# Both directions of a delta rule head solved in one product of 128 rows

## The chip, the cores and the metric

One core of a Trainium2 chip. The metric is the device time of one launch in microseconds. The core has a matrix engine (TensorE, PE in the profile, with its weight loads as PEld), a vector engine (DVE), an activation engine (ACT), GpSimd (POOL), and a queue that issues most DMAs (SP). TensorE writes to PSUM only, from which DVE and ACT read.

## The reference, cut to what matters

One encoder layer over two sequences of 256 tokens (512 rows, 1024 channels, f32): RMSNorm, one wide projection, three branches (a bidirectional gated delta rule with 8 heads of 128, latent attention with 8 heads, cross attention into 256 memory tokens), their gated sum, an output projection and a last RMSNorm. The change touches the delta rule, which each head computes in both directions:

```python
lmat = einsum("nbhck,nbhek->nbhce", kb, kc) * decay * (1.0 - eye)
t_inv = triangular_solve(lmat + eye, eye)        # unit lower triangular
u = einsum("nbhce,nbhev->nbhcv", t_inv, vc * bc)
w = einsum("nbhce,nbhek->nbhck", t_inv, kb * exp(gc))
...
v_new = u_i - w_i @ state
o = (q_i * exp(g_i)) @ state + (q_i k_i^T * decay_i) @ v_new
state = state * exp(g_last) + (k_i * exp(g_last - g_i))^T @ v_new
...
o_gdn = rmsnorm(o_fwd + o_bwd) * silu(z)
```

The backward direction is the same on the reversed sequence. The kernel does not go chunk by chunk with a state: it solves the triangular system of a whole sequence of 256 tokens by blocks and multiplies the result (`ub`) with the decayed products of q and k.

## The kernel before, in words

`run` (L1210) has three stages. `front` computes the memory branch, the norms, the projections and the latent attention. `middle` computes the delta rule heads while TensorE works through projections. `back` computes the last branch product (`gm_bg`) and the output (`y`). Long products are `gemm` (L220): f32 inputs are split into two rounded parts, and three products of 128x128 by 128x512 for each slice of 128 input channels give one output tile. Each weight tile comes by a DMA (`wr`), is copied on ACT (`wh`) and subtracted on DVE or GpSimd (`wl`), with two buffers each.

In `middle` the order of TensorE's instructions is written by hand: `weave` (L1375) runs several generators against a clock of its own. Each `yield a, b` says that the generator has just issued `a` us of TensorE work and wants to go on `b` us later; until then `weave` issues instructions of the long products (`self.fill`), 0.234 us each. The instructions of the other engines are placed by the compiler's scheduler; every engine takes its own in order. The generators are `preps` (two of `gdn_prep`, each for four heads), `heads_load` and `heads_in` (decays, products of k and q), two of `lane` (even and odd heads; each runs `gdn_solve` for its heads, one after the other) and `heads_out` (`gdn_out`). `can` holds back the fill work whose inputs are not there; `load_xa` brings the attention branch's results back from DRAM into buffers of the solve that have come free.

The solve of a head has 256 tokens in two chunks of 128 for each of two sequences (`s`) and two directions (`d`). `gdn_prep` inverts diagonal blocks of 32 on DVE. With them `gdn_solve` (L912) makes inverses of 64:

- `p1` and `yp` (L933, L944), each 16 products of 32x32, give the corner blocks between two inverses of 32; ACT copies `p1` to `p1s` and `yp` into `y64` (L954). The forward direction has its first half in partitions 0 to 63 and its second in 64 to 127; the backward direction has them the other way round.
- Then for `cp` 0 and 1 (first and second chunk of a direction): `u` (L984) multiplies the inverse of the first half by its part of v, ACT copies it into `ub` (L988), `xs` (L997) multiplies the block between the halves (from `na`) by it, DVE subtracts that from v (`w2`, L1001), `us` (L1009) multiplies by the second half's inverse, ACT copies into `ub` (L1013). Each of the three is four products of 64x64 by 64x128, one for each sequence and direction, with the directions on different quarters of the array.
- Between `cp` 0 and 1, `x` (L973), four products of 128x128 by 128x128, and a subtraction from v on DVE (L976).

All of these products are in f32, not split. `vt` (`vs` in the profile) is the head's v, loaded from DRAM by one DMA (L845) and scaled by `nk` (L908). `y64` has, for each direction, sequence and chunk, 64 rows of an inverse in each partition half; its four copies from `o1` and `o2` (L827) mask one half with `hm`.

Of the kernel before, what the change touches and what calls it, by code (L numbers as in the profile page):

```python
# [40 lines left out]
def _consts():  # L41
    t = np.arange(P)
    b = t // 32
    same = b[:, None] == b[None, :]
    le = t[:, None] <= t[None, :]
    ge = t[:, None] >= t[None, :]
    z, o = np.zeros((P, P)), np.ones((P, P))
    a8 = np.arange(8)
    anc = np.zeros((P, 2, 2, 8))
    for tb in range(2):  # L50
        tg = tb * P + t
        anc[:, 0, tb] = tg[:, None] >= 32 * a8[None]
        anc[:, 1, tb] = tg[:, None] < 32 * (a8[None] + 1)
    i32 = np.arange(32)
    m = (t % 32)[:, None]
    parts = [
        ("id", np.eye(P)), ("bd", same),
        ("anc", anc.reshape(P, 32)),
        ("trf", m <= i32), ("trb", m >= i32), ("i32", m == i32),
        ("ngf", np.where(i32 > m, 0.0, NEG)), ("ngb", np.where(i32 < m, 0.0, NEG)),  # L60
        ("hm", np.stack([b % 2 == 0, b % 2 == 1], 1)),
        ("one", np.ones((P, 1))), ("hf", np.full((P, 64), -0.5)), ("ph", np.full((P, 16), 0.5)),
    ]
# [92 lines left out]
class Layer:  # L156
# [558 lines left out]
    def gdn_prep(self, g, kqs):  # L715
# [58 lines left out]
        nc.vector.tensor_scalar(nk, nk, 0.25, None, ALU.mult)  # L774
        self.cn[g] = cc, nk
# [40 lines left out]
        y64 = pg.tile([P, 32, 64], F32, tag="y64", bufs=2, name=f"y64{g}")  # L816
# [6 lines left out]
        for d in range(2):  # L823
            u = slice(16 * d, 16 * d + 16)
            ysrc = o1 if d else o2
            for hf in range(2):
                nc.scalar.activation(y64[:, u, 32 * hf:32 * hf + 32], ysrc[:, :, u].rearrange("p i u -> p u i"),  # L827
                                     AF.Copy, scale=c("hm")[:, hf:hf + 1])
                if g:
                    yield 0.0, 2.5  # L830
        self.ready[g] = self.now + (10 if g else 80)
        return t32, y64, cc

    def decay_in(self, hh):
        nc, pg = self.nc, self.pg

        es = []
        for d in range(2):
            e = pg.tile([P, 2, 384], F32, tag="e", bufs=6, name=f"e{hh}{d}")
            for a in range(4):  # L840
                src = self.d_r[d, 4 * hh + a:4 * hh + a + 1].rearrange("a s i -> a (s i)")
                nc.sync.dma_start(e[32 * a:32 * a + 32].rearrange("p s i -> p (s i)"), src.to_broadcast([32, 768]))
            es.append(e)
        vt = self.s2(f"vs{hh}")
        nc.sync.dma_start(vt, self.d_v[:, hh])  # L845
        return es, vt
# [65 lines left out]
    def gdn_solve(self, hh):  # L912

        nc, pg, c = self.nc, self.pg, self.c
        t32, y64, cc = self.pr[hh // 4]
        h, par = hh % 4, hh % 2
        na, es, vt = self.hd[hh]
        v4 = vt.rearrange("p (s c d) -> p s c d", s=2, c=2)

        def ncol(d, s, cch):  # L920

            cp = cch if d == 0 else 1 - cch
            return (256 if cp else (128 if d else 0))
# [3 lines left out]
        for j in range(4):  # L927
            s, cch = j // 2, j % 2
            for m in range(2):
                for d in range(2):  # L930
                    f, sb = (2 * m + 1, 2 * m) if d else (2 * m, 2 * m + 1)
                    n0 = ncol(d, s, cch) + 32 * sb
# [3 lines left out]
        p1s = pg.tile([P, 128], F32, tag="p1", bufs=2, name=f"p1s{hh}")  # L936
# [3 lines left out]
        for j in range(4):  # L940
            for m in range(2):
                for d in range(2):
                    f, sb = (2 * m + 1, 2 * m) if d else (2 * m, 2 * m + 1)
                    nc.tensor.matmul(yp[32 * f:32 * f + 32, 32 * j:32 * j + 32],  # L944
                                     p1s[32 * sb:32 * sb + 32, 32 * j:32 * j + 32],
                                     y64[32 * sb:32 * sb + 32, 16 * d + 4 * h + j, 32 * (1 - d):32 * (1 - d) + 32],
                                     start=True, stop=True)
        for d in range(2):
            for m in range(2):
                f = 2 * m + 1 if d else 2 * m  # L950
                r = slice(32 * f, 32 * f + 32)
                dst = y64[r, 16 * d + 4 * h:16 * d + 4 * h + 4, 32 * (1 - d):32 * (1 - d) + 32]
                src = yp[r, 0:128].rearrange("p (j i) -> p j i", j=4)
                nc.scalar.activation(dst, src, AF.Copy)  # L954
# [4 lines left out]

        def half(d, first):  # L960
            return slice(64, 128) if (d == 1) == first else slice(0, 64)

        for cp in range(2):
            def vin(d, r):
                return v4[r, :, d if cp == 0 else 1 - d]

            if cp == 1:
# [7 lines left out]
                for d in range(2):  # L975
                    nc.vector.tensor_tensor(v4[:, :, 1 - d], v4[:, :, 1 - d], x4[:, d], op=ALU.subtract)  # L976
                yield 0.9, 5.0
            up = self.ps_ms(par, f"u{hh}{cp}")
            u3 = up[:, 0:256].rearrange("p (s e) -> p s e", s=2)
            for s in range(2):  # L980
                for d in range(2):
                    r = half(d, True)
                    cch = cp if d == 0 else 1 - cp
                    nc.tensor.matmul(u3[r, s], y64[r, 16 * d + 4 * h + 2 * s + cch], vin(d, r)[:, s],  # L984
                                     start=True, stop=True)
            for d in range(2):
                r = half(d, True)
                nc.scalar.activation(ub[r, d, :, cp], u3[r], AF.Copy)  # L988
            yield 0.58, 5.0
            xp = self.ps_ms(par, f"xs{hh}{cp}")  # L990
            x3 = xp[:, 0:256].rearrange("p (s e) -> p s e", s=2)
            for s in range(2):
                for d in range(2):
                    f, sb = half(d, True), half(d, False)
                    cch = cp if d == 0 else 1 - cp
                    n0 = ncol(d, s, cch) + sb.start
                    nc.tensor.matmul(x3[sb, s], na[f, d, s, n0:n0 + 64], ub[f, d, s, cp], start=True, stop=True)  # L997
            w2 = pg.tile([P, 2, P], F32, tag=f"w2{par}", bufs=1, name=f"w2{hh}{cp}")
            for d in range(2):
                sb = half(d, False)  # L1000
                nc.vector.tensor_tensor(w2[sb], vin(d, sb), x3[sb], op=ALU.subtract)  # L1001
            yield 0.58, 5.0
            up = self.ps_ms(par, f"us{hh}{cp}")
            u3 = up[:, 0:256].rearrange("p (s e) -> p s e", s=2)
            for s in range(2):
                for d in range(2):
                    sb = half(d, False)
                    cch = cp if d == 0 else 1 - cp
                    nc.tensor.matmul(u3[sb, s], y64[sb, 16 * d + 4 * h + 2 * s + cch], w2[sb, s],  # L1009
                                     start=True, stop=True)  # L1010
            for d in range(2):
                sb = half(d, False)
                nc.scalar.activation(ub[sb, d, :, cp], u3[sb], AF.Copy)  # L1013
            yield 0.58, 5.0
        self.ub[hh] = ub

    def gdn_out(self, hh):
# [29 lines left out]
        yield 0.0, 9  # L1047
# [193 lines left out]
    def plan(self):  # L1241
# [12 lines left out]
        xa = [(f, n) for n in range(5) for f in (self.load_xa, self.split_xa)]  # L1254
# [65 lines left out]
    def middle(self):  # L1320
# [5 lines left out]
        nc.vector.memset(self.tt.rearrange("p a b -> p (a b)")[:, 0:1024:33], 1.0)  # L1326
        self.loads, self.loaded, self.started = {}, {}, set()
# [38 lines left out]
    def can(self, f, *a):  # L1366

        if f == self.load_xa:
            return (3 in self.ub and self.pr[1], 5 in self.ub and 7 in self.hd, 6 in self.ub and 7 in self.hd,
                    self.out > 6 and 7 in self.started, 7 in self.ub)[a[0]]  # L1370
# [58 lines left out]
    def load_xa(self, part):  # L1429

        lo, hi = ((0, 2), (2, 3), (3, 4), (4, 5), (5, 8))[part]
        ts = []
        while lo + len(ts) < hi:
            f = lo + len(ts)
            if f in (0, 6):
                t = self.pg.tile([P, 2, 2, 512], F32R, tag="y64", bufs=2, name=f"xa{f}")
                ts += [t[:, 0], t[:, 1]]
            else:
                t, n = ("ub", 2) if f == 4 else ("na", 3)
                ts.append(self.pg.tile([P, 2, 512], F32R, tag=t, bufs=n, name=f"xa{f}"))  # L1440
        for f, t in enumerate(ts, lo):
            self.nc.sync.dma_start(t[:, 1].bitcast(F32), self.d_xa[:, f])
        self.xa_at[part] = self.now + 6.0 if part < 4 else self.now
# [33 lines left out]
```

## Time and profile before

| | before |
|---|---|
| time, median of 3 runs | 902.44 us (900.96 to 902.75) |
| profiled execution, its own time | 902.51 us |
| its span, first to last instruction | 900.6 us |
| granted TensorE clock, mean | 0.993 |
| busy: PE, PEld, DVE, ACT, POOL | 98%, 78%, 65%, 48%, 22% |

How to read it: the shares are of the span, over all stages. The name of a product is its output tile, with the line that issued it; `gm_` names are the long products. An instruction's duration for PE runs from its start to its modelled end, and the next one starts before that end; what an instruction costs in a busy stream is the difference between starts. An f32 product stands as two MATMUL records, a split one as one. Some matmul records can be missing, so a row may count one fewer than were issued.

### The profile page before, as it was taken

How to read it: one execution, taken by the hardware profiler on the slowest of the kernel's cores; microseconds unless marked ns; L12 is line 12 of the kernel's file. 1: busy time of each engine (PE TensorE's matmuls, PEld its weight loads, DVE VectorE, ACT ScalarE, POOL GpSimd, SP SyncE). 2: the span in 40 equal slices, each digit the busy share in tenths (PEclk: the TensorE clock that was granted, in tenths of full speed). 3: DMA queues.
4: the chain of work that ended last, by engine and by line, in shares of the span. 5: the costliest groups of instructions: out<-in, count | busy, mean ns of one | idle time of the engine just before them, and what ended most of it. 6: DMA issues, size and time to landing. Idle time of an engine off the chain costs nothing.

```text
span 900.6 us, 13529 instructions
## 1 busy us (share of the span) xinstructions
PE 879.4 (98%) x5100; PEld 706.2 (78%) x5100; DVE 584.3 (65%) x988; ACT 432.0 (48%) x769; POOL 197.9 (22%) x146
## 2 busy tenths in 40 slices
PE   7999999999999999999989998999999999999997
PEld 5878886888888888887867776777777778888886
DVE  6775447876678774489979995575655445336642
ACT  6655445554554544364375368555553333213332
POOL 0230341222122200060230232431220000332221
PEclk9999999999999999999989999999999999999999
DMA  9322211532335433364322345443432337455422
GB/s 333 115 86 84 90 58 52 160 103 89 97 96 150 138 103 121 117 188 142 126 97 83 129 129 152 143 122 124 129 107 96 100 102 242 163 183 207 123 96 94
DMA packets 47520, 114.03 MB, mean 127 GB/s; under 512 B 6496, under 2 KB 9696, under 8 KB 47456
## 3 DMA queue, kind: packets, MB, share of 16 engines
q1 hardware_dynamic: 42704, 104.52, 36.7%
q10 hardware_dynamic: 4752, 8.65, 2.6%
q8 instruction: 40, 0.66, 0.3%
q14 instruction: 24, 0.20, 0.1%
HBM read 93.03 MB, written 16.97 MB: 122 GB/s over the span
## 4 chain that ended last, share of the span: by engine, by line
PE 91%; ACT 4%; DVE 1%; DMA 1%; issue 1%; POOL 0%; SPq 0%; POOLq 0%; ACTq 0%; DVEq 0%
PE gm_g L232 15%; PE gm_qkv L232 14%; PE gm_z L232 6%; PE gm_bm L232 5%; PE gm_bg L232 5%; PE gm_za L232 5%; PE y L1158 5%; PE vm L359 3%; PE gm_be L232 3%; PE gm_qm L232 3%; PE gm_km L232 2%; PE kk L895 2%; PE s_a L282 2%; PE o L1034 2%; PE gm_cq L232 2%; PE gm_qn L232 2%
## 5 line engine op out<-in xcount | busy, mean ns | idle before, releaser
L205 POOL TENSOR_TENSOR wl_qkv<-wr_qkv,wh_qkv 128x1024 fp32r<-128x1024 f32 x24 | 59.7, 2489 | 152.9 <-ACT wh_qkv L201 49.7
L686 DVE SCALAR_TENSOR_TENSOR kq<-cz,prm,kq 128x510 f32<-128x510 f32 (+1 forms) x64 | 55.2, 862 | 10.3 <-ACT kq L679 9.4
L232 PE MATMUL gm_qkv<-hh,wh_qkv 128*128 128x512 f32 x192 | 52.3, 408 | 0.1
L232 PE MATMUL gm_qkv<-hh,wl_qkv 128*128 128x512 f32 x192 | 52.2, 406 | 0.0
L232 PE MATMUL gm_g<-hh,wh_g 128*128 128x512 f32 x192 | 51.7, 403 | 0.0
L232 PE MATMUL gm_g<-hh,wl_g 128*128 128x512 f32 x192 | 51.4, 399 | 0.0
L232 PE MATMUL gm_g<-hl,wh_g 128*128 128x512 f32 x192 | 51.0, 400 | 0.0
L232 PE MATMUL gm_qkv<-hl,wh_qkv 128*128 128x512 f32 x192 | 50.6, 399 | 0.0
L1128 POOL TENSOR_TENSOR mg<-mg,lg 128x512 f32<-128x512 f32 x16 | 28.0, 1749 | 75.9 <-DVE lg L1127 75.9
L205 DVE TENSOR_TENSOR wl_g<-wr_g,wh_g 128x1024 fp32r<-128x1024 f32 x24 | 29.9, 1247 | 22.4 <-ACT wh_g L201 11.0
L232 PEld LDWEIGHTS gm_qkv<-hh,wh_qkv 128*128 128x128 f32 x192 | 36.0, 193 | 9.8 <-issue 0.9
L885 POOL TENSOR_TENSOR kl<-kq,kh 128x512 fp32r<-128x512 f32 x16 | 20.7, 1296 | 101.4 <-ACT kh L883 101.4
L232 PEld LDWEIGHTS gm_qkv<-hl,wh_qkv 128*128 128x128 f32 x192 | 35.6, 188 | 9.3 <-issue 1.1
L232 PEld LDWEIGHTS gm_g<-hl,wh_g 128*128 128x128 f32 x192 | 35.7, 188 | 9.0 <-issue 0.9
L232 PEld LDWEIGHTS gm_g<-hh,wl_g 128*128 128x128 f32 x192 | 35.8, 188 | 8.8 <-issue 0.7
L232 PEld LDWEIGHTS gm_g<-hh,wh_g 128*128 128x128 f32 x192 | 35.4, 189 | 8.8 <-issue 1.0
L232 PEld LDWEIGHTS gm_qkv<-hh,wl_qkv 128*128 128x128 f32 x192 | 35.8, 192 | 8.2 <-issue 0.3
L1158 PE MATMUL y<-wh_wo,mh 128*128 128x512 f32 (+1 forms) x144 | 39.7, 368 | 0.0
L201 ACT ACTIVATE wh_g<-wr_g 128x1024 fp32r<-128x1024 f32 x24 | 25.4, 1057 | 27.2 <-PE gm_g L232 19.3
L201 ACT ACTIVATE wh_qkv<-wr_qkv 128x1024 fp32r<-128x1024 f32 x24 | 25.4, 1057 | 23.8 <-PE gm_qkv L232 6.5
L798 DVE TENSOR_TENSOR tm<-xx,tt 128x1 f32<-128x1 f32 (+30 forms) x62 | 34.7, 560 | 1.3
L232 PE MATMUL gm_bm<-xa,wh_bm 128*128 128x512 f32 x128 | 32.6, 397 | 0.0
(396 smaller groups left out, 2220.6 us busy)
## 6 DMA issues: line engine op xcount, KB each, us to landing
wr_qkv<-in_w_dram SPq DMA_DIRECT2D x24, 512.0 KB, 3.5
wr_g<-in_w_dram SPq DMA_DIRECT2D x24, 512.0 KB, 3.6
e<-d_r SPq DMA_DIRECT2D x64, 96.0 KB, 3.0
wr_z<-in_w_dram SPq DMA_DIRECT2D x12, 512.0 KB, 3.9
wr_za<-in_w_dram SPq DMA_DIRECT2D x8, 512.0 KB, 3.5
d_g<-gt_g ACTq DMA_DIRECT2D x16, 256.0 KB, 2.1
wr_bm<-in_w_dram SPq DMA_DIRECT2D x8, 512.0 KB, 3.6
lg<-d_g SPq DMA_DIRECT2D x16, 256.0 KB, 3.5
```

What stands on the lines that cost most here:

```text
L201: nc.scalar.activation(hi[:, :n], raw[:, :n], AF.Copy)
L205: eng.tensor_tensor(lo[:, :n], raw[:, :n], hi[:, :n].bitcast(F32), op=ALU.subtract)
L232: nc.tensor.matmul(ps[:m], a[:, k * m:(k + 1) * m], xs[k][j], start=n == 0, stop=n == 3 * nk - 1)
L282: nc.tensor.matmul(sp[:, qb * 256:(qb + 1) * 256], a, b, start=j == 0, stop=j == n - 1)
L359: nc.tensor.matmul(vps[tb], ms[k][a][:, t], b[:, :512], start=k == 0 and i == 0, stop=k == 7 and i == 2)
L686: nc.vector.scalar_tensor_tensor(ys, zs, self.cw[:, f, m:m + 1], ys, ALU.mult, ALU.add)
L798: nc.vector.tensor_tensor(t3, xx[:, i:i + 1, 0:i].to_broadcast([P, i, i]), tt[:, 0:i, 0:i], op=ALU.mult)
L885: nc.gpsimd.tensor_tensor(lo, src, hi.bitcast(F32), op=ALU.subtract)
L895: nc.tensor.matmul(ps, a[:, k], b, start=i == 0, stop=i == 2)
L1034: nc.tensor.matmul(out, ub[:, d, s, cp], rhs, start=n == 0, stop=n == 3)
L1128: nc.gpsimd.tensor_tensor(self.merged[d], self.merged[d], gt, op=ALU.add)
L1158: nc.tensor.matmul(ps, xs[2 * j + q][a][:, t], b[:, q * 512 + c0:q * 512 + c1], start=j == 0 and n == 0, stop=j == 3 and n == 5)
```

## The change

The two directions are put into one operand. A tile `y` of 128x128 per sequence and chunk holds, on its diagonal, the 64x64 inverse of the forward direction's first half (partitions 0 to 63) and of the backward direction's first half (64 to 127); a second one holds the second halves. The rest of `y` is zeroed once per lane. So `u` and `us` are two products of 128x128 by 128x128 (one for each sequence) in place of four of 64x64. For `xs`, a tile `m` of 128x128 holds the two blocks between the halves on its off-diagonal quarters, copied from `na`; the rest is zero. So that both directions stand at the same chunk index, partitions 64 to 127 of v (and of its scale `nk`, now `ns`) are loaded with their chunks swapped, which takes three DMAs. `y64` becomes `y32` (without `hm`), and `y` is put together on ACT in each head: eight copies of diagonal blocks, four of corner blocks, two for `m` (`between`) and two more for the second chunk. The result of `u` is copied whole into `u2` for `xs`, and then by halves into `ub` as before. The yields of the solve are smaller. Since `y64` is gone, `load_xa` uses other buffers in six parts in place of five, the order of `gm_bm` leaves the last two slices of its input to the end in place of the last three, and the last head's `gdn_out` waits 13 in place of 9.

```diff
-        last = {"bm": 5, "bg": 7, "qm": 4}.get(name[:2])
+        last = {"bm": 6, "bg": 7, "qm": 4}.get(name[:2])
...
-        nc.vector.tensor_scalar(nk, nk, 0.25, None, ALU.mult)
-        self.cn[g] = cc, nk
+        ns = col("ns")
+        nc.vector.tensor_scalar(ns[0:64], nk[0:64], 0.25, None, ALU.mult)
+        for q in range(2):
+            nc.vector.tensor_scalar(ns[64:128, q::2], nk[64:128, 1 - q::2], 0.25, None, ALU.mult)
+        self.cn[g] = cc, ns
...
+        nc.scalar.activation(y32[:, 0:16], o2[:, :, 0:16].rearrange("p i u -> p u i"), AF.Copy)
+        if g:
+            yield 0.0, 2.5
+        for q in range(2):
+            nc.scalar.activation(y32[:, 16 + q:32:2], o1[:, :, 17 - q:32:2].rearrange("p i u -> p u i"), AF.Copy)
+            if g:
+                yield 0.0, 1.5
...
-        nc.sync.dma_start(vt, self.d_v[:, hh])
+        nc.sync.dma_start(vt[0:64], self.d_v[0:64, hh])
+        to, fr = (a.rearrange("p (s c d) -> p s c d", s=2, c=2) for a in (vt[64:128], self.d_v[64:128, hh]))
+        for q in range(2):
+            nc.sync.dma_start(to[:, :, q], fr[:, :, 1 - q])
...
+        def between(cp):
+            for d in range(2):
+                f, sb = (slice(64, 128), slice(0, 64)) if d else (slice(0, 64), slice(64, 128))
+                n0 = ncol(d, cp) + sb.start
+                nc.scalar.activation(m[f, :, sb], na[f, d, :, n0:n0 + 64], AF.Copy)
...
+        for i in range(2):
+            for q in range(2):
+                d = q ^ i
+                for f in (2 * q, 2 * q + 1):
+                    nc.scalar.activation(blk(i, f, f), y32[32 * f:32 * f + 32, 16 * d + 4 * h:16 * d + 4 * h + 4], AF.Copy)
+        for i in range(2):
+            for q in range(2):
+                f, g = (2 * q + 1, 2 * q) if q ^ i else (2 * q, 2 * q + 1)
+                nc.scalar.activation(blk(i, f, g), yp[32 * f:32 * f + 32, 0:128].rearrange("p (j i) -> p j i", j=4),
+                                     AF.Copy)
+        between(0)
         yield 0.32, 5.5
...
-                for d in range(2):
-                    nc.vector.tensor_tensor(v4[:, :, 1 - d], v4[:, :, 1 - d], x4[:, d], op=ALU.subtract)
-                yield 0.9, 5.0
+                for q in (1, 0):
+                    for r in range(2):
+                        t, d = slice(64 * r, 64 * r + 64), r ^ q ^ 1
+                        nc.vector.tensor_tensor(v4[t, :, q], v4[t, :, q], x4[t, d], op=ALU.subtract)
+                yield 0.9, 4.5 if hh > 2 else 5.0
...
-                for d in range(2):
-                    r = half(d, True)
-                    cch = cp if d == 0 else 1 - cp
-                    nc.tensor.matmul(u3[r, s], y64[r, 16 * d + 4 * h + 2 * s + cch], vin(d, r)[:, s],
-                                     start=True, stop=True)
+                nc.tensor.matmul(u3[:, s], y[:, 0, 2 * s + cp], v4[:, s, cp], start=True, stop=True)
+            u2 = w2(f"u2{hh}{cp}")
+            nc.scalar.activation(u2, u3, AF.Copy)
             for d in range(2):
-                r = half(d, True)
-                nc.scalar.activation(ub[r, d, :, cp], u3[r], AF.Copy)
-            yield 0.58, 5.0
+                t = slice(64 * d, 64 * d + 64)
+                nc.scalar.activation(ub[t, d, :, cp], u3[t], AF.Copy)
+            yield 0.45, 4.5 if hh > 2 else 5.0
...
+                nc.tensor.matmul(x3[:, s], m[:, s], u2[:, s], start=True, stop=True)
+            if cp == 0:
+                between(1)
+            wv = w2(f"w2{hh}{cp}")
+            nc.vector.tensor_tensor(wv, v4[:, :, 1 - cp], x3, op=ALU.subtract)
+            yield 0.45, 4.5 if hh > 2 else 5.0
...
+                nc.tensor.matmul(u3[:, s], y[:, 1, 2 * s + cp], wv[:, s], start=True, stop=True)
...
-        yield 0.0, 9
+        yield 0.0, 13 if hh == 7 else 9
...
+            y = self.pg.tile([P, 2, 4, P], F32, tag=f"y{j}", bufs=1, name=f"y{j}")
+            m = self.pg.tile([P, 2, P], F32, tag=f"m{j}", bufs=1, name=f"m{j}")
+            nc.gpsimd.memset(y, 0.0)
+            nc.gpsimd.memset(m, 0.0)
...
-        lo, hi = ((0, 2), (2, 3), (3, 4), (4, 5), (5, 8))[part]
+        lo, tags = ((0, ("y32",)), (1, ("na",)), (2, ("na", "y0")), (4, ("y32",)), (5, ("ub",)), (6, ("na", "y1")))[part]
```

## Rows read from the trace of the kernel before

**Rows 1.** The page: busy time of each engine, TensorE's granted clock in 40 slices of the span (tenths), and the chain that ended last by engine.

```profile
PE 879.4 (98%) x5100; PEld 706.2 (78%) x5100; DVE 584.3 (65%) x988; ACT 432.0 (48%) x769; POOL 197.9 (22%) x146
...
PEclk9999999999999999999989999999999999999999
...
PE 91%; ACT 4%; DVE 1%; DMA 1%; issue 1%; POOL 0%; SPq 0%; POOLq 0%; ACTq 0%; DVEq 0%
```

**Rows 2.** The view of waits, of PE: who waited for whom, us in total, times, the longest.

```profile
PE p L933 <- ACT t L820: 3.7, 2, 2.9
PE kk L895 <- DVE e L906: 2.3, 2, 2.0
PE vp L708 <- DVE og L1058: 1.0, 1, 1.0
```

**Rows 3.** The view of windows, three stretches: from:to and length, then busy us (instructions) of PE, PEld, DVE, ACT and POOL, the granted clock, the DMA share and GB/s.

```profile
470.50:477.30 6.80, 6.80 (x25) 5.06 (x25) 4.28 (x7) 4.87 (x8) 0.00 (x0) 0.70 0.25 81
...
490.00:560.00 70.00, 68.57 (x443) 53.06 (x439) 57.06 (x85) 39.95 (x64) 17.04 (x12) 1.00 0.42 133
...
600.00:755.00 155.00, 155.00 (x1113) 121.30 (x1114) 79.95 (x153) 68.42 (x138) 22.16 (x22) 1.00 0.38 116
```

**Rows 4.** The view of groups by form, of PE: rows and columns of the stationary operand, the moving one, records, busy us, mean ns.

```profile
L984 PE MATMUL u<-vs,y 64*64 64x128 f32 x128 | 10.7, 290 | 0.0
```

**Rows 5.** The timeline of PE from 640 to 672 us: start, us, the line and its product, records.

```profile
650.35 0.97 PE L232 MATMUL gm_g<-hh,wh_g 128*128 128x512 f32 x3
651.16 1.05 PE L268 MATMUL rob<-cst,ro 128*128 128x128 f32 x8
651.97 0.95 PE L232 MATMUL gm_g<-hh,wh_g 128*128 128x512 f32 x3
652.75 1.80 PE L232 MATMUL gm_g<-hl,wh_g 128*128 128x512 f32 x7
654.48 0.65 PE L997 MATMUL xs<-ub,na 64*64 64x128 f32 x8
...
660.46 0.65 PE L1009 MATMUL us<-w,y 64*64 64x128 f32 x8
661.04 1.20 PE L232 MATMUL gm_be<-xe,wh_be 128*128 128x512 f32 x4
662.09 0.40 PE L232 MATMUL gm_be<-xe,wl_be 128*128 128x512 f32 x1
...
667.91 2.04 PE L232 MATMUL gm_g<-hh,wh_g 128*128 128x512 f32 x8
669.79 2.04 PE L232 MATMUL gm_g<-hl,wh_g 128*128 128x512 f32 x8
```

**Rows 6.** The timeline of PE again, around 483 and 500 us, where the two lanes go side by side.

```profile
483.53 1.09 PE L984 MATMUL u<-vs,y 64*64 64x128 f32 x16
484.55 0.50 PE L232 MATMUL gm_z<-hl,wh_z 128*128 128x512 f32 x1
...
500.44 1.95 PE L973 MATMUL x<-ub,na 128*128 128x128 f32 x16
502.22 0.60 PE L708 MATMUL vp<-cst,vf 128*128 128x128 f32 x4
502.58 2.12 PE L232 MATMUL gm_z<-hh,wh_z 128*128 128x512 f32 x8
```

**Rows 7.** The view of groups by form, of ACT, from 455 to 760 us.

```profile
L988 ACT ACTIVATE ub<-u 64x256 f32<-64x256 f32 x32 | 12.0, 376 | 6.2 <-PE u L984 5.7
...
L827 ACT ACTIVATE y<-o,cst 128x512 f32<-128x512 f32 x8 | 9.2, 1194 | 0.1
...
L954 ACT ACTIVATE y<-yp 32x128 f32<-32x128 f32 x32 | 8.5, 266 | 5.7 <-PE yp L944 5.3
```

**Rows 8.** The timeline of PE around 711 us: `yp` of head 7, and its first `u`.

```profile
710.65 0.45 PE L944 MATMUL yp<-y,p1s 32*32 32x32 f32 x32
...
717.09 0.65 PE L984 MATMUL u<-vs,y 64*64 64x128 f32 x8
```

**Rows 9.** The timeline of ACT before the first `p`.

```profile
464.11 2.29 ACT L827 ACTIVATE y<-o,cst 128x512 f32<-128x512 f32 x2
```

**Rows 10.** The view of groups by form, of DVE, from 455 to 760 us.

```profile
L1001 DVE TENSOR_TENSOR w<-vs,xs 64x256 f32<-64x256 f32 x32 | 13.4, 418 | 8.4 <-PE xs L997 7.7
...
L976 DVE TENSOR_TENSOR vs<-vs,x 128x256 f32<-128x256 f32 x16 | 6.0, 415 | 2.3 <-PE x L973 2.2
```

**Rows 11.** The timeline of SP around 632 us: DMA issues, merged.

```profile
632.50 2.64 SPq L842 DMA_DIRECT2D e<-d_r  x6
```

**Rows 12.** The view of DMA issues: KB each, median us from issue to landing.

```profile
vs<-d_v SPq DMA_DIRECT2D x8, 256.0 KB, 4.2
```

**Rows 13.** The page's costliest groups: one of GpSimd.

```profile
L205 POOL TENSOR_TENSOR wl_qkv<-wr_qkv,wh_qkv 128x1024 fp32r<-128x1024 f32 x24 | 59.7, 2489 | 152.9 <-ACT wh_qkv L201 49.7
```

**Rows 14.** The timeline of PE from 700 us: the last `us`, and the `o` of head 7.

```profile
752.85 0.65 PE L1009 MATMUL us<-w,y 64*64 64x128 f32 x8
...
755.40 2.78 PE L1034 MATMUL o<-e,ub 128*128 128x256 f32 x16
```

**Rows 15.** The timeline of PE after the wait of `p`.

```profile
472.47 3.00 PE L232 MATMUL gm_qkv<-hh,wh_qkv 128*128 128x512 f32 x8
475.31 2.03 PE L232 MATMUL gm_qkv<-hl,wh_qkv 128*128 128x512 f32 x8
```

More of the change, by code (lines that the diff above doesn't have):

```diff
@@ L822, in gdn_prep @@
                 yield 0.0, 1.5
-        for d in range(2):
[L824 to L830, printed above, removed]
+        nc.scalar.activation(y32[:, 0:16], o2[:, :, 0:16].rearrange("p i u -> p u i"), AF.Copy)
[5 more added lines that the diff above has]
+                yield 0.0, 1.5
         self.ready[g] = self.now + (10 if g else 80)
-        return t32, y64, cc
+        return t32, y32, cc
     def decay_in(self, hh):
@@ L928, in gdn_solve @@
             s, cch = j // 2, j % 2
[L929 removed]
+            for q in range(2):
                 for d in range(2):
[L931 to L932 removed]
+                    f, sb = (2 * q + 1, 2 * q) if d else (2 * q, 2 * q + 1)
+                    n0 = ncol(d, 1 - cch if d else cch) + 32 * sb
                     nc.tensor.matmul(p1[32 * sb:32 * sb + 32, 32 * j:32 * j + 32],
@@ L1005, in gdn_solve @@
             for s in range(2):
[L1006 to L1010, printed above, removed]
+                nc.tensor.matmul(u3[:, s], y[:, 1, 2 * s + cp], wv[:, s], start=True, stop=True)
             for d in range(2):
-                sb = half(d, False)
-                nc.scalar.activation(ub[sb, d, :, cp], u3[sb], AF.Copy)
-            yield 0.58, 5.0
+                t = slice(64 * (1 - d), 64 * (1 - d) + 64)
+                nc.scalar.activation(ub[t, d, :, cp], u3[t], AF.Copy)
+            yield 0.45, 4.5 if hh > 2 else 5.0
         self.ub[hh] = ub
@@ L1253, in plan @@
         self.xe, self.xa, self.xa_at, self.xa_raw, A = [], [None] * 8, {}, {}, self.A
-        xa = [(f, n) for n in range(5) for f in (self.load_xa, self.split_xa)]
+        xa = [(f, n) for n in range(6) for f in (self.load_xa, self.split_xa)]
         g = [(self.gate_tile, j, d) for j in (0, 1) for d in range(8)]
@@ L1326, in middle @@
         nc.vector.memset(self.tt.rearrange("p a b -> p (a b)")[:, 0:1024:33], 1.0)
+        self.ym = []
+        for j in range(2):
+            y = self.pg.tile([P, 2, 4, P], F32, tag=f"y{j}", bufs=1, name=f"y{j}")
+            m = self.pg.tile([P, 2, P], F32, tag=f"m{j}", bufs=1, name=f"m{j}")
+            nc.gpsimd.memset(y, 0.0)
+            nc.gpsimd.memset(m, 0.0)
+            self.ym.append((y, m))
         self.loads, self.loaded, self.started = {}, {}, set()
@@ L1369, in can @@
             return (3 in self.ub and self.pr[1], 5 in self.ub and 7 in self.hd, 6 in self.ub and 7 in self.hd,
-                    self.out > 6 and 7 in self.started, 7 in self.ub)[a[0]]
+                    7 in self.started, self.out > 6 and 7 in self.started, 7 in self.ub)[a[0]]
         if f == self.split_xa:
@@ L1429, in load_xa @@
     def load_xa(self, part):
-        lo, hi = ((0, 2), (2, 3), (3, 4), (4, 5), (5, 8))[part]
[L1432 to L1440, printed above, removed]
+        lo, tags = ((0, ("y32",)), (1, ("na",)), (2, ("na", "y0")), (4, ("y32",)), (5, ("ub",)), (6, ("na", "y1")))[part]
+        ts = [self.pg.tile([P, 2, 512], F32R, tag=t, bufs={"na": 3, "y0": 1, "y1": 1}.get(t, 2), name=f"xa{f}")
+              for f, t in enumerate(tags, lo)]
         for f, t in enumerate(ts, lo):
             self.nc.sync.dma_start(t[:, 1].bitcast(F32), self.d_xa[:, f])
-        self.xa_at[part] = self.now + 6.0 if part < 4 else self.now
+        self.xa_at[part] = self.now + 6.0 if part < 5 else self.now
         self.xa_raw[part] = ts, lo
```

49 lines of the change are left out of this document (16 added, 33 removed).

## The prediction

> **What bounds the kernel now.** I read the head of the page first [rows 1]. TensorE (PE) is busy for 98% of the 900.6 us span at nearly full clock, and 91% of the chain that ended last is PE work. So what leaves PE's ordered stream leaves the time, unless a new wait opens. The view of waits says where PE stood still: before the first `p` products, at a `kk` and at a `vp` [rows 2], 7.0 us together. From 600 to 755 us, where half of the solves run, the windows show PE busy for all 155.00 us, with ScalarE (ACT) busy for 68.42 [rows 3].
>
> In this stretch the stream is the long `gemm` products, at 0.234 us an instruction, into which `weave` drops small groups of head work. An f32 product is two MATMUL records: `u` has 128 for 8 heads of 8 products [rows 4]. The mean of 290 ns there is latency and no price, since products overlap. I price by differences of starts, so a group's price is its own length plus what its neighbours lose.
>
> **The products.** Each head has six groups (`u`, `xs`, `us`, for two chunks) of four 64x64 products, 8 records; after the change a group is two 128x128 products, 4 records. `p`, `yp`, `x`, `o` keep their count.
>
> A 64x64 group in the timeline [rows 5]: `us` starts at 660.46, the next product at 661.04: 0.58. The seven long products before `xs` (652.75 to 654.48) take 1.73 where 7 x 0.234 = 1.64: 0.09 lost at the entry. The four after `us` (661.04 to 662.09) take 1.05 for 0.94: 0.11 lost at the exit. The plain pace is 669.79 - 667.91 = 1.88 for 8. Together 0.58 + 0.09 + 0.11 = 0.78.
>
> A full-size f32 group, `rob`, 8 records of the form the change uses [rows 5]: 651.97 - 651.16 = 0.81. The three products before it take 0.81 as well, 0.11 over pace, but those follow a 64x64 group and that is its exit loss; so the entry costs 0. The three after (651.97 to 652.75) take 0.78 for 0.70: 0.08. In [rows 6], four full-size records, `vp`, hold PE for 502.58 - 502.22 = 0.36. So the new group costs 0.36 + 0.08 = 0.44, and a group saves 0.78 - 0.44 = 0.34.
>
> The saving is not in the arithmetic. In [rows 6] sixteen 64x64 records take 484.55 - 483.53 = 1.02, so the second eight add 0.44, just what four full records cost at the pace of `x` (502.22 - 500.44 = 1.78 for 16, 0.11 each). Two 64x64 products on different quarters already run side by side. What goes is what surrounds a 64x64 group: entry, exit and the 0.14 that the first eight take over the second.
>
> The Trainium skill, TensorEngine Tiling (Array Packing), Key Properties, says both things: tiles of one mode work independently, and a change of mode drains TensorE. The first speaks against this change, since by it alone nothing is gained and the sum stays at 902.5; the second is what the entry and exit rows show, and by the two together the sum is the one below.
>
> The sum: of 48 groups, six stand in three back-to-back pairs of lanes (as at 483.53), where 0.09 + 1.02 + 0.11 = 1.22 becomes 0.81 + 0.08 = 0.89: 3 x 0.33 = 1.0 us. The other 42 give 42 x 0.34 = 14.3. I counted 16 sides of these that touch not a long product but other small f32 work, where an entry or exit may stay: at most 16 x 0.10 = 1.6 less. I take 1.0 less: **14.3 us saved**, between 0 (if the losses stay with any small f32 group) and 15.7.
>
> **ACT.** Per head it gains 8 diagonal-block copies, 4 copies of `between` and 2 full copies `u2`; its 4 + 8 others stay. The nearest rows are 266 ns for 32x128 and 376 ns for 64x256 [rows 7]: 12 x 0.27 + 2 x 0.38 = 4.0 us a head, 32 us in all. The four `y` copies of a `gdn_prep` at 1.194 become one of that size and two of half: 4.8 becomes about 2.4, 5 less in all. Net +27 us, beside PE, on an engine busy 57% of 490 to 560 and 44% of 600 to 755 [rows 3]: priced at 0. The cover is the gap that `weave` leaves before the next stage. For the longest list, between `yp` and `u`, that is 717.09 - 710.65 = 6.4 us [rows 8] for 14 copies, 3.7 us. Only the 4 corner copies need `yp`; the others wait for nothing that is late. If all 14 queue up behind it, see the rivals. In the `u` stage the path gets shorter: one full copy lets `xs` go, where two half copies stood.
>
> At the first `p` (PE idle 3.7 us [rows 2]) the order on ACT is two `t` copies, two `y` copies of 2.29 us together, then the last two `t` copies that PE waits for [rows 9]. With half-size `y` copies there the wait may end 1 us sooner. Against it, heads 0 and 1 both put 16 diagonal and 4 `between` copies (5.4 us) on ACT before their `u` at 483.53, with room, by windows 470.5 to 477.3, of 6.80 - 4.87 = 1.9 us in that part alone. I set -1 and +1: 0, bounds -3 and +3.
>
> **VectorE (DVE).** `w` goes from two 64x256 operations to one 128x256, 2 x 0.418 to 0.415, twice a head; the subtraction from `v` goes from two 128x256 to four 64x256, 2 x 0.415 to 4 x 0.418 [rows 10]. These cancel. Three column operations for one in each `gdn_prep` are 128x16 and small: 0.
>
> **SP, DMA, GpSimd.** The load of `vs` becomes three DMAs, two with 512-byte rows. SP issues `e` DMAs at 2.64 / 6 = 0.44 us [rows 11], so a head holds SP 0.9 us longer; behind it stand weight loads, which go a buffer ahead, and `heads_in` only comes 9 us after the issue, where landing takes 4.2 [rows 12]. Hidden; uncovered, 8 x 0.9 = 7. GpSimd gets four memsets ahead of the middle. No row shows one; the nearest operation, 128x1024 with two inputs, is 2.49 us [rows 13], so 0 to 6 us, on a queue with slack. 0.
>
> **Order of the stream.** The yields fall from 0.58 to 0.45 and, from head 3, from 5.0 to 4.5, so stages come closer: less time for each copy. At the end the head chain and the fill before `gm_bm` run out together: the last `us` is at 752.85 and `o` already at 755.40 [rows 14], 2.6 us later where 5.0 were asked for, so filling had run out. Both shrink (six stages of head 7 by 0.63 each, PE's own work by 14), and the smaller `xa` pieces with `last` at 6 give the final load three more products to hide under. 0, bounds -2 and +3.
>
> **Sum.** 902.5 (profiled execution; span 900.6, so 1.9 outside it) - 14.3 = 888.2; the median of the runs is 902.44, so nothing is to be added. I say **888**.
>
> **The rivals.**
> - *Nothing gained.* The entry and exit belong to any group of f32 products that is this short, and the halved count saves nothing since pairs run side by side. For: 0.44 against 0.44 above. Against: the zero entry of `rob` and the 0.36 of four `vp` records. 902, chance 0.04. This is also the case in which the change doesn't do what its words say.
> - *More gained.* The pile of `t` and `y` copies on ACT at both preps shrinks, and with it the waits of `kk` and `vp` (3.3) [rows 2], 1 us at `p`, and part of the slow clock: in 470.5 to 477.3 the granted clock is 0.70 on average [rows 3], its low level of 1.2 GHz for a part, after PE had idled; 8 products take 475.31 - 472.47 = 2.84 there [rows 15], 1.0 over pace. 888 - 3.3 - 1 - 2 = 882. For: the copies stand there in a row. Against: other work may fill the room. 0.16.
> - *Less gained.* Stages at 4.5 find ACT at a weight split or a prep copy; 40 stages of heads 3 to 7 with 0.15 us each, 6 us: 894. Against: PE shows no wait at these lines now. 0.13.
> - *Slower.* The 14 copies all stand behind `yp`, so `u` waits for an assembled `y`: 3.7 us of copies, stretched by ACT's other work to 3.7 / 0.43 = 8.6 us in heads 0 to 3 and 3.7 / 0.56 = 6.6 in heads 4 to 7, against 6.4 of cover: 4 x 2.2 + 4 x 0.2 = 9.6 us. With the `ub` copies of the other lane in front (2 x 0.38) and the lane's next five stages each late by 0.1 to 0.2, 15 us, and after four of these waits a slow stretch as above, 4 x 2 us more: 888 + 15 + 8 = 911. It decides from a wait of about 2 us a head. For: ACT is the busier engine here. Against: diagonal copies can run as soon as the lane's earlier `us` is done. 0.08.
>
> **How the numbers follow.** Forecast 0.59 (883 to 893), the rivals 0.16, 0.13, 0.04, 0.08. For 8 in 10 the range goes over more and less gained with their bounds: 880 to 897. Within 0.2% is 1.8 us, about what a measurement of this kernel can tell from no change: faster 0.88, same 0.04, slower 0.08.
>
> **What would show it.** Right: `u`, `xs`, `us` have 64 records each in 128x128 form, four of them take 0.36, the product before keeps 0.23, PE's busy time falls by about 14, its waits at `p`, `kk` and `vp` stay near 7 us. Wrong: long products still at 0.33 ahead of the new groups (nothing gained); PE waits at `u` for ACT `y`, or at `xs` for ACT `u2` or `m` (less gained, slower); a clock under 0.99 after such waits.

## The result and the profile after

The changed kernel takes 893.92 us in the median of 4 runs (892.01 to 894.78), the kernel before 902.18 us of 4 beside it; the ratio is 0.9907, 95% interval 0.9888 to 0.9927. So 8 us are gained where 14 were forecast. The time lies 1 us outside the 883 to 893 of the forecast itself and inside the wider range of 880 to 897, next to the 894 of the rival "less gained". The profiled execution took 892.01 us, span 890.2, the fastest of the four.

The head of the page of the changed kernel, against [rows 1]: busy time of each engine.

```profile
PE 864.7 (97%) x4908; PEld 708.5 (80%) x4908; DVE 588.5 (66%) x992; ACT 456.9 (51%) x879; POOL 205.1 (23%) x150
```

PE's busy time fell by 14.7 us, with 192 records less, but the span by 10.4. ACT's rose by 24.9 (27 were forecast). The rest is in the view of waits of PE, against [rows 2]:

```profile
...
PE p L952 <- ACT t L823: 2.7, 2, 1.8
PE gm_qkv L231 <- DVE zt_z L1081: 2.5, 2, 1.6
PE us L1024 <- ACT vt L710: 1.6, 1, 1.6
PE pt_a L304 <- DVE p_a L300: 1.5, 2, 1.3
PE kk L901 <- DVE e L912: 1.4, 1, 1.4
...
```

In this execution `p` waits 1.0 less (in the repeat, run 1 below, it waits 3.7 as before); the wait of `vp` (1.0) is gone; but `us` and a long product (for DVE's `zt_z`, which must empty its PSUM buffer) wait anew, and `pt_a`, which is in `front`, waits 1.0 more. The groups by form show the product in its new form, 64 records against 128 in [rows 4]:

```profile
L1005 PE MATMUL u<-vs,y 128*128 128x128 f32 x64 | 9.7, 277 | 0.2 <-ACT y L981 0.2
```

In the timeline, the stretch in which a `u` and a `us` stand between long products:

```profile
645.50 1.05 PE L267 MATMUL rob<-cst,ro 128*128 128x128 f32 x8
646.31 1.41 PE L231 MATMUL gm_g<-hl,wh_g 128*128 128x512 f32 x5
647.56 0.61 PE L1005 MATMUL u<-vs,y 128*128 128x128 f32 x4
647.92 0.94 PE L231 MATMUL gm_g<-hl,wh_g 128*128 128x512 f32 x3
648.70 0.61 PE L1024 MATMUL us<-w,y 128*128 128x128 f32 x4
649.06 1.41 PE L231 MATMUL gm_g<-hh,wl_g 128*128 128x512 f32 x5
...
651.70 0.86 PE L231 MATMUL gm_g<-hh,wl_g 128*128 128x512 f32 x3
```

A group holds PE for 647.92 - 647.56 = 0.36. The three products between the groups take 648.70 - 647.92 = 0.78, 0.08 over pace, which is the exit. At the entry, the five ahead of `u` take 647.56 - 646.31 = 1.25 for 1.17, the 0.08 that is the exit of `rob`, and the three ahead of `us` take no more than that exit: the entry costs nothing. That is the 0.44 of the prediction, here in its place.

### The profile page after: what moved, and what is told of

It is laid out like the page before. It is cut to its first block, busy times and chain, and to the rows that moved or that the text cites. A ratio compares the mean times of both kernels' runs of the same rounds, so it can differ in the third digit from the quotient of the medians.

```text
span 890.2 us, 13288 instructions
## 1 busy us (share of the span) xinstructions
PE 864.7 (97%) x4908; PEld 708.5 (80%) x4908; DVE 588.5 (66%) x992; ACT 456.9 (51%) x879; POOL 205.1 (23%) x150
## 5 line engine op out<-in xcount | busy, mean ns | idle before, releaser
L800 DVE TENSOR_TENSOR tm<-xx,tt 128x1 f32<-128x1 f32 (+30 forms) x62 | 37.0, 597 | 1.2
L891 POOL TENSOR_TENSOR kl<-kq,kh 128x512 fp32r<-128x512 f32 x16 | 23.7, 1484 | 53.0 <-ACT kh L889 53.0
L685 DVE SCALAR_TENSOR_TENSOR vf<-cz,prm,vf 128x510 f32<-128x510 f32 (+1 forms) x32 | 29.6, 925 | 7.4 <-ACT vf L678 7.1
```

The source lines that it names most:

```text
L685: nc.vector.scalar_tensor_tensor(ys, zs, self.cw[:, f, m:m + 1], ys, ALU.mult, ALU.add)
L800: nc.vector.tensor_tensor(t3, xx[:, i:i + 1, 0:i].to_broadcast([P, i, i]), tt[:, 0:i, 0:i], op=ALU.mult)
L891: nc.gpsimd.tensor_tensor(lo, src, hi.bitcast(F32), op=ALU.subtract)
```

## The experiments

All times are medians; ratios are to the kernel before, run beside it on the same chip (902.83 us for runs 1 to 4, 902.68 for runs 5 to 8, 902.64 for runs 9 to 12). The *middle* is the stretch from the first `kd` to the first `gm_bm` product in the timeline of PE: 757.93 - 382.36 = 375.6 us before, 746.38 - 384.06 = 362.3 after.

**1. The changed kernel again.** No edit.

> The changed kernel once more, nothing edited. Edge theory (a group of 64x64 products costs 0.34 us more than a group of two full ones, in what it and its neighbours lose, and the rest of the change is about neutral): the middle, from the first kd product to the first gm_bm product, again about 13 us shorter than before. If the 1.7 us that the stage ahead of the middle took longer in the profiled execution is scatter, it comes out within 1 us of before here and the time near 892; if it belongs to the change, it stays at +1.7 and the time at 894.

895.4 us, ratio 0.9921 (0.9907 to 0.9934). In its profile, an execution of 894.08 us, the middle is 364.6 long and starts at 383.85, so the stage ahead of it is again 1.5 us longer than before: that belongs to the change and is not scatter. The granted clock of this execution is 0.993 on average, as in that of before, where the first profile of the changed kernel has 0.996; so I use this one for the accounts below. The same kernel, in the same order, thus differs by 2.3 us in the middle between two executions. One place is `p`: here ACT's preparation copies ahead of it wait 0.57 and 0.28 for DVE, in the first profile they don't, and `p` waits 3.7 against 2.7. The granted clock from 460 to 480 us is 0.83 here, as before the change, and 0.91 in the first profile; from 560 to 580 us it is 0.91 here and before, and 1.00 in the first profile.

**2. The products undone, all else kept.**

```diff
-                nc.tensor.matmul(u3[:, s], y[:, 0, 2 * s + cp], v4[:, s, cp], start=True, stop=True)
+                for d in range(2):
+                    r = slice(64 * d, 64 * d + 64)
+                    nc.tensor.matmul(u3[r, s], y[r, 0, 2 * s + cp, r], v4[r, s, cp], start=True, stop=True)
```

and likewise `xs` and `us`, each with its own quarters.

> The changed kernel with u, xs and us again as four 64x64 products each, read from the quarters of y and m; same order, same copies, same yields, only the product form is undone. Edge theory: +0.34 x 42 and 0.32 x 3, less up to 1, so 14 us more than the changed kernel (about 908). Count theory (a price of 0.11 per record, 8 records for 4): +0.44 x 48 = 21 us (915). Rival that the gain lies in the order and the yields and not in the products: within 3 us of the changed kernel.

904.96 us, ratio 1.003 (1.0018 to 1.0041): 9.6 over run 1 and 11.0 over the first measurement, where 14 were expected. The page shows PE busy for 880.3 us against 867.2 in run 1, 13.1 more, of which 12.2 lie in the middle; PE's idle time in the middle fell from 8.9 to 6.9 at the same time.

**3. The full products executed twice.**

```diff
+                for _ in range(2):
-                nc.tensor.matmul(x3[:, s], m[:, s], u2[:, s], start=True, stop=True)
+                    nc.tensor.matmul(x3[:, s], m[:, s], u2[:, s], start=True, stop=True)
```

and likewise `u` and `us`.

> The changed kernel with each of the 96 full products of u, xs and us executed twice, into the same place. It has the same 8 records in a group as the quarters, but in full form. Edge theory: a full record costs its 0.11 and nothing at the edges, so 4 x 0.11 x 48 = 21 us more than the changed kernel (915), that is 7 more than the quarters of the same count. Count theory: as the quarters, 21 each. Rival that small products hide in waits: under 10.

918.15 us, ratio 1.0171 (1.0157 to 1.0185), 22.8 over run 1, where 21 were expected; PE busy 888.2, 21.0 more.

The order of PE's instructions is the same in the three kernels, so the stretch shown above can be laid beside theirs. With the quarters:

```profile
652.48 1.05 PE L267 MATMUL rob<-cst,ro 128*128 128x128 f32 x8
653.29 1.41 PE L231 MATMUL gm_g<-hl,wh_g 128*128 128x512 f32 x5
654.63 0.65 PE L1007 MATMUL u<-vs,y 64*64 64x128 f32 x8
655.22 0.96 PE L231 MATMUL gm_g<-hl,wh_g 128*128 128x512 f32 x3
656.10 0.65 PE L1030 MATMUL us<-w,y 64*64 64x128 f32 x8
...
659.35 0.86 PE L231 MATMUL gm_g<-hh,wl_g 128*128 128x512 f32 x3
```

And with the full products twice:

```profile
661.95 1.05 PE L267 MATMUL rob<-cst,ro 128*128 128x128 f32 x8
...
664.00 1.05 PE L1006 MATMUL u<-vs,y 128*128 128x128 f32 x8
664.81 0.94 PE L231 MATMUL gm_g<-hl,wh_g 128*128 128x512 f32 x3
...
669.04 0.86 PE L231 MATMUL gm_g<-hh,wl_g 128*128 128x512 f32 x3
```

From `rob` to the last row it takes 651.70 - 645.50 = 6.20 us after, 659.35 - 652.48 = 6.87 with the quarters, 669.04 - 661.95 = 7.09 with double full products. Per group the quarters cost (6.87 - 6.20) / 2 = 0.34 more, and four more full records (7.09 - 6.20) / 2 = 0.45. Of the 0.34, the rows show 0.09 at the entry (five products in 1.34 where they take 1.25 after) and 0.59 - 0.36 = 0.23 in the group. Eight quarter records in a group take 0.59, eight full ones 0.81: by the record the quarters are the cheaper. The count theory, 21 us for either, is out.

One stretch could be chance, but the same holds for all groups behind 600 us. From the first `u` there to the first `gm_bm`, 27 groups long, PE never waits and its granted clock is 1.00 (columns as in [rows 3]), in run 1, with the quarters and with double full products:

```profile
609.73:748.46 138.73, 138.73 (x938) 116.81 (x937) 76.64 (x142) 78.22 (x179) 17.53 (x19) 1.00 0.40 123
612.01:759.77 147.76, 147.76 (x1046) 114.37 (x1046) 76.53 (x142) 78.20 (x179) 17.46 (x19) 1.00 0.37 116
620.52:771.31 150.79, 150.79 (x1046) 128.88 (x1045) 77.68 (x142) 78.52 (x179) 17.45 (x19) 1.00 0.36 113
```

The first profile of the changed kernel also takes 138.73 for it (607.65 to 746.38). Per group that is (147.76 - 138.73) / 27 = 0.33 for the quarters and (150.79 - 138.73) / 27 = 0.45 for four more full records. So the edge theory gets both prices of a group. The time of run 2 came out below its 14 all the same: of the 10.2 us that its middle grew over run 1, 9.0 lie here, and the 21 groups ahead of 600 us, which stand among waits and changes of the clock, add 1.2.

The Trainium skill, TensorEngine Tiling (Array Packing), Key Properties, states that a change of tiling mode drains TensorE. The rows agree with that in so far as 0.09 us are lost ahead of a group of quarters and 0.23 in it; whether the 0.23 are such a drain or another cost of a short group of quarters, its weight loads for one, no run here separates.

**4. Yields of 5.0 in the changed kernel.**

```diff
-                yield 0.9, 4.5 if hh > 2 else 5.0
+                yield 0.9, 5.0
```

in all four places of the solve.

> The changed kernel with 5.0 in place of 4.5 in the four yields of heads 3 to 7, so that every stage has as long as before for its copies. If the closer stages cost waits for ACT and DVE: 1 to 4 us less than the changed kernel. If closer stages are what the shorter head chain lives on: 1 to 4 us more, with PE idle near the end of the middle. If neither: within 1 us.

901.91 us, ratio 0.9993 (0.9982 to 1.0005): 6.5 over run 1: nearly all of the gain is gone, though PE's busy time is 869.3, still 10 under before. The end of its middle, in the timeline of PE:

```profile
746.95 0.60 PE L1024 MATMUL us<-w,y 128*128 128x128 f32 x4
747.39 0.60 PE L1048 MATMUL o<-e,ub 128*128 128x256 f32 x2
748.25 2.45 PE L1048 MATMUL o<-e,ub 128*128 128x128 f32 x14 [0.26 <-ACT ub L1027]
754.26 1.05 PE L1064 MATMUL so<-cst,sq 128*128 128x1 f32 x8 [3.56 <-DVE sq L1060]
755.18 4.59 PE L231 MATMUL gm_bm<-xa,wh_bm 128*128 128x512 f32 x12
```

Behind the last `us` there is no long product left: `o` and `so` stand bare and wait, and only then comes `gm_bm`. In the changed kernel the same place is filled, as in [rows 14]:

```profile
740.12 0.61 PE L1024 MATMUL us<-w,y 128*128 128x128 f32 x4
740.49 0.71 PE L231 MATMUL gm_g<-hh,wl_g 128*128 128x512 f32 x2
...
743.85 2.78 PE L1048 MATMUL o<-e,ub 128*128 128x256 f32 x16
746.38 3.05 PE L231 MATMUL gm_bm<-xa,wh_bm 128*128 128x512 f32 x12
```

**5. The new yields alone, in the kernel before.**

```diff
-            yield 0.58, 5.0
+            yield 0.45, 4.5 if hh > 2 else 5.0
```

in three places, with 4.5 after `x` and 13 in the last `gdn_out`.

> The kernel before with the new yields alone (0.45 for 0.58, 4.5 for 5.0 from head 3 on, 13 for 9 after the last head); products, copies and loads as before. The run with 5.0 in the changed kernel lost 6.5 us because the head chain then outlasts the fill. Pair theory (the shorter stages are worth something only once PE has less to do, since before the chain and the fill end together): within 2 us of before. Rival (the shorter stages bring the 8 us by themselves): 894 to 897. Second rival (copies come late at 4.5): 1 to 4 us over before.

904.52 us, ratio 1.002 (1.0011 to 1.0029). The gain is the pair's: the changed kernel with 5.0 throughout brings 0.9 us (run 4, which keeps the other new yields), the new yields with the old products cost 1.8, both bring 7.4 (run 1). One wait of PE is new in it (those of `kk` and `vp` in [rows 2] are gone), and ACT's timeline at that place shows why:

```profile
PE gm_z L232 <- DVE zt_z L1067: 5.0, 1, 5.0
```

```profile
542.31 2.28 ACT L820 ACTIVATE t<-o 32x512 f32<-32x512 f32 x2
544.61 2.39 ACT L827 ACTIVATE y<-o,cst 128x512 f32<-128x512 f32 x2
547.01 2.17 ACT L820 ACTIVATE t<-o 32x512 f32<-32x512 f32 x2
549.19 2.19 ACT L827 ACTIVATE y<-o,cst 128x512 f32<-128x512 f32 x2
551.41 0.60 ACT L1066 ACTIVATE zt_z<-gm_z 128x512 f32<-128x512 f32 x1
```

Nine microseconds of `t` and `y` copies of the second `gdn_prep` stand ahead of `zt_z`, without which a long product's PSUM buffer is not free. That is the pile of the rival "more gained". The changed kernel's `y` copies are shorter, 4.8 us against 9.2 for both calls of `gdn_prep` [rows 7]:

```profile
L977 ACT ACTIVATE y<-y 32x128 f32<-32x128 f32 x64 | 18.7, 304 | 0.6
...
L830 ACT ACTIVATE y<-o 128x256 f32<-128x256 f32 x4 | 2.5, 669 | 0.0
L826 ACT ACTIVATE y<-o 128x512 f32<-128x512 f32 x2 | 2.3, 1134 | 0.0
```

**6. Without the diagonal copies from head 2 on.**

```diff
-                for f in (2 * q, 2 * q + 1):
+                for f in (2 * q, 2 * q + 1) if hh < 2 else ():
```

> The changed kernel without the eight copies of diagonal blocks in heads 2 to 7 (they keep those of heads 0 and 1, so these heads' results are not the reference's); 48 ACT copies of 0.27 us, 13 us of ACT, are left out. If ACT's added work makes the waits of 4 to 5 us that PE has in the middle of the changed kernel and not before: 2 to 4 us less than the changed kernel. If the copies lie in ACT's idle time: within 1 us of it.

892.89 us, ratio 0.9888 (0.9876 to 0.9901), 1.0 below the first measurement of the changed kernel and 2.5 below the second. The waits of `us` and of the long product near 552 and 572 us stay (1.59 and 1.56 long). So these 48 of the 64 copies cost between nothing and 2.5 us, and don't make the new waits.

**7. The diagonal copies on GpSimd.**

```diff
-                    nc.scalar.activation(blk(i, f, f), y32[...], AF.Copy)
+                    nc.gpsimd.tensor_copy(blk(i, f, f), y32[...])
```

> The changed kernel with the eight diagonal copies of each head on GpSimd in place of ACT. If ACT is what is short: 1 to 4 us less than the changed kernel. If GpSimd, in order, holds them behind a weight subtraction of 2.5 us or holds its own work behind them: PE waits at u for y, 1 to 6 us more. If neither: within 1 us.

893.98 us, ratio 0.9904 (0.9891 to 0.9917), within 1.5 us of the changed kernel: ACT is 18 us freer, and the time does not follow. The wait of `us` for `vt` is gone here, but a long product waits 2.6 for `zt_z`, `rob` 1.6 for GpSimd's `ro` and `x` 1.1 in its place.

**8. Yields of 4.0 from head 3 on.** The edit of run 4 with 4.0 in place of 4.5.

> The changed kernel with 4.0 in place of 4.5 from head 3 on. From 5.0 to 4.5 the time fell by 6.5 us. If the head chain still ends the middle at 4.5 (o of head 7 comes 3.7 us after the last us where 4.5 + 0.45 were asked for, so about 1.2 us without fill): up to 1.5 us less. If ACT and DVE are now late: 1 to 4 us more.

895.52 us, ratio 0.9918 (0.9903 to 0.9934), no difference to run 1. Still closer stages in these heads bring nothing more.

**9. One DMA for v.** The four lines of the diff that load `vt` replaced by the one of before.

> The changed kernel with v loaded by one DMA a head as before; the chunks of partitions 64 to 127 are then not swapped, so the backward direction works on the wrong chunk and only the time is read. The stage ahead of the middle takes 1.0 to 1.4 us longer in all seven profiles of the changed form, in a wait of pt_a near 317 us, and there the first loads of v have moved on SP. If the three DMAs make that wait: it is under 0.4 us here, and the time 1 to 2 us less. If the order on DVE comes from elsewhere: the wait stays at 1.0 to 1.4 and the time within 1 us of the changed kernel.

892.42 us, ratio 0.9881 (0.9865 to 0.9897). In the view of waits:

```profile
PE pt_a L304 <- DVE p_a L300: 0.5, 2, 0.3
```

The wait near 317 us is gone, and the middle starts at 382.19, as before the change (382.36). So the 1.5 us in `front`, ahead of every changed product, come from the three DMAs. The traces show the way. On ACT of run 9 the copy `cz` stands ahead of the weight copy `wh_za`, as in the kernel before:

```profile
303.45 0.63 ACT L686 ACTIVATE cz<-kq 128x512 f32<-128x512 f32 x1 [4.31 <-DVE kq L685]
303.99 1.04 ACT L200 ACTIVATE wh_za<-wr_za 128x1024 fp32r<-128x1024 f32 x1
```

In the changed kernel it stands behind it, `wh_za` waits for the landing of its weights, and DVE, from which `pt_a` needs `p_a` later, waits for `cz`:

```profile
304.25 1.06 ACT L200 ACTIVATE wh_za<-wr_za 128x1024 fp32r<-128x1024 f32 x1 [4.31 <-DMA wr_za<-in_w_dram]
305.21 0.61 ACT L686 ACTIVATE cz<-kq 128x512 f32<-128x512 f32 x1
...
305.86 0.69 DVE L687 SCALAR_TENSOR_TENSOR kq<-cz,kq 128x512 f32<-128x512 f32 x1 [1.64 <-ACT cz L686]
```

The three DMAs are the only edit between the two, so it is they that made the compiler's scheduler put these two copies in another order.

**10. The copy `ts` of the second preparation on GpSimd.**

```diff
+        if g:
+            nc.gpsimd.tensor_copy(ts, tt.rearrange("p c r -> p r c"))
+        else:
-        nc.scalar.activation(ts, tt.rearrange("p c r -> p r c"), AF.Copy)
+            nc.scalar.activation(ts, tt.rearrange("p c r -> p r c"), AF.Copy)
```

> The changed kernel with one copy of the second gdn_prep (ts, 2.05 us on ACT) on GpSimd. In the changed kernel ACT takes its instructions in order, stood 2.63 us for DVE at this copy and then ran it, and the copy of vp that PE's us at 550 waits for (1.57 us) stood behind it. If this is the wait: it goes, with up to 1.6 us of time. If the wait only moves to the next instruction: within 1 us.

It is aimed at this part of the changed kernel's timeline of ACT, with the `us` of PE that waited 1.56 us until 549.89:

```profile
546.84 2.05 ACT L806 ACTIVATE ts<-tt 128x1024 f32<-128x1024 f32 x1 [2.63 <-DVE tt L802]
548.79 0.57 ACT L1106 ACTIVATE gt_g<-gm_g 128x512 f32<-128x512 f32 x1
549.27 0.57 ACT L710 ACTIVATE vt<-vp 128x512 f32<-128x512 f32 x1
```

ACT stood 2.63 us for DVE's last reduction, since it takes its instructions in order; the copy of `vp` (`vt`), which frees a PSUM buffer, ran at 549.27, though that product had started at 544.83. With `ts` on GpSimd: 890.55 us, ratio 0.9869 (0.9852 to 0.9885), 3.4 and 4.9 us under the two measurements of the changed kernel. The wait for `vt` is gone, a new one of `rob` for GpSimd is there:

```profile
PE p L955 <- ACT t L826: 2.6, 2, 1.9
PE rob L267 <- POOL ro L1070: 1.4, 1, 1.4
PE pt_a L304 <- DVE p_a L300: 1.4, 2, 1.2
PE xs L1018 <- ACT u L1010: 1.1, 1, 1.1
...
PE gm_qkv L231 <- DVE zt_z L1084: 0.8, 2, 0.6
```

The gain is more than the 1.6 us that were expected at most. The wait for `zt_z` is 1.4 shorter than in run 1 as well; that of `p` is 1.1 shorter, but that happened in the first profile of the unedited kernel too. The rest of the gain is not traced.

**11. Yields of 4.5 for all heads.**

```diff
-                yield 0.9, 4.5 if hh > 2 else 5.0
+                yield 0.9, 4.5
```

> The changed kernel with 4.5 for all heads, also 0 to 2. If the head chain's length in the middle is what counts: the chain is up to 3 us shorter, the time 0 to 2 us less. If heads 0 to 2 are held by the preparation of the inverses and by ACT near 470 to 550: new waits at u and us, 0 to 3 us more.

891.0 us, ratio 0.9868 (0.9851 to 0.9885), as good as run 10. Here too the waits of `us` for `vt` and of the long product are gone; in their place `kk` waits 2.0, `so` 1.5 and `xs` 1.1. So the same gain comes without touching `ts`, by other instructions meeting near 550 us.

**12. Both kinds of copy on GpSimd.** The edits of runs 7 and 10 together.

> The changed kernel with both the eight diagonal copies and that ts copy on GpSimd. If ACT's added work is what the middle waits for: 2 to 3 us less than the changed kernel, about 891 to 892. If the waits only move to other places, as the diagonal copies alone let expect (893.98): 893 to 895.

892.82 us, ratio 0.9885 (0.9866 to 0.9903): no better than run 10 alone. A new wait of 2.6 us (a long product for `zt_z`, near 543 us) takes the place of the old, and `us` waits 0.9 for `vt` again, with `ts` off ACT.

## Why the prediction was right, and where it was off

**The mechanism holds.** The 0.34 us of a group, taken from rows of before, is the 0.33 that the 27 groups behind 600 us cost in run 2; it lies at the entry and in a group of 64x64 products and not in the number of products, which run 3 shows by adding records. The rival "nothing gained" is out. The allowance of 1.0 for groups beside other small work was not needed: six of the 27 stand beside `kk`, `o` or `rob` and cost, by starts, 0.33 to 0.35 like the rest. (The upper bound of 15.7 does not follow from its terms; they add up to 14.3 + 1.0 = 15.3.)

**The sum of 14.3 was nearly met in the middle.** Undoing the products alone moves PE's busy time in the middle by 12.2 (run 2 against run 1). Against the kernel before, the middle of run 1 is 375.6 - 364.6 = 11.0 us shorter; PE's idle time in it, by starts against modelled ends, is 8.9 where it was 7.0. So without waits the middle got 12.9 shorter, 1.4 less than the term. The missing 1.4 is not in the price of the groups behind 600 us; where it is, no run shows.

**The step that failed is the price of 0 for what surrounds the products.** In the account of run 1 (span 892.3 against 900.6): -12.9 for the products and what goes with them, +1.9 for waits in the middle, +1.5 in `front`, and +1.2 behind the middle (885.05 - 748.46 = 136.6 from the first `gm_bm` to the last product where it was 135.9, and 0.5 after it), together -8.3. The 1.5 in `front` are the three DMAs (run 9). I had looked for their cost on SP and in the landing; it came by the order that the scheduler makes.

Of the waits in the middle one is traced: `us` for `vt` behind `ts` on ACT, a copy of the second preparation (run 10). The new copies on ACT are not shown to be its cause: taking most of them away (run 6) leaves it, moving them (run 7) trades it for others. The rival "less gained" named a preparation copy too, but in the stages that come 4.5 apart, from head 3 on. There it was wrong: this wait is 1.6 with 5.0 (run 4) and with 4.0 (run 8) in those heads as well, and in the 138.73 us that hold most of those stages PE waits nowhere.

Of the 1.2 behind the middle, 0.7 lie in the pace of products that the change does not touch. By starts, `gm_bm`, `gm_bg` and `y` take 46.84, 44.98 and 44.77 where they took 46.68, 44.79 and 44.43, without a wait and at a granted clock of 1.00 in both. The last two are within 0.01 of that in every profile of the changed form, and within 0.03 of the old numbers in run 5; the cause stays open. The 0.5 is scatter: from the start of the last product to the end of the span the profiles of the changed form have 6.8 to 7.6, the kernel before 6.8.

**What was luck.** The point of 888 was missed by 6 us, and the range held because the rivals had widened it, one of them to 894 by a loss of 0.15 us in each of 40 stages that the runs don't show. PE's waits at `p`, `kk` and `vp`, which were to stay near 7 us, fell to 4.4 in run 1, and waits elsewhere more than took their place.

**ACT's cover held.** 24.9 us of work more, at 304 ns a diagonal copy where I took 266, and no wait at `u` for `y` above 0.2 us. The slower rival did not come near its condition, a wait of about 2 us a head at `u`.

**The order of the stream** was priced at 0 with the yields as they are, with bounds of -2 and +3. What hangs on those yields is more than that: run 4 puts it at 6.5 us. Without the shorter stages the chain of heads outlasts the fill, and the PE time that is saved turns into a bare end of the middle. My sentence that "both shrink" was right, but it held up nearly half of the forecast, and I spent one line on it.

**The scatter.** Executions of the changed kernel run from 892.0 to 896.0; the two that were profiled differ by 2.1 us in time, at a mean granted clock of 0.996 and 0.993. One median is not good to 1 us here.

## What to carry to other kernels

Where a full engine's stream alternates long products with short groups, price a group by the starts around it, with what the neighbours lose, not by its records: two products on quarters may cost as little as one full one, and their edges still more than the product. And when a change takes time from the engine that fills a schedule, ask what else has a length of its own there: here the chain of heads had to be shortened too, or the saving is given back at the end (run 4). For a wait behind an engine that takes its instructions in order, look at the instruction that stands at its head: moving `ts`, 2 us of work, went with 3 to 5 us, and moving 18 us of other copies with nothing. That is one run; run 11 got as much by other yields, and run 12, with both moved, did not add to it.

## What the runs showed of the hardware that I had not expected

Eight records of 64x64 products on different quarters take 0.59 us as a group and eight full ones 0.81, in the same place of the same stream; but four full ones, which do the same work, take 0.36, and ahead of them nothing is lost. The products `gm_bg` and `y` of `back`, which the change does not touch, ran 0.4 and 0.8% slower in every profile of the changed form (44.98 and 44.77 us for 44.79 and 44.43), at a granted clock of 1.00; no run shows why. A change that only splits one load into three moved instructions of another engine in a stage that it does not touch, by way of the compiler's order, and cost 1.5 us there.
